# The gathered expert rows of the last token block, moved out of the building of the routing grid

## The chip, the core and the metric

One core of a Trainium2 chip runs the whole decoder layer in one launch. The metric is the time of one execution in device microseconds, and the median of three executions is compared. A span is the time from the first to the last instruction of one profiled execution, so that execution's own time lies a little above its span.

## The reference, cut to what matters

The layer runs a mixer of two attention branches, a cross-attention to memory tokens, and then the PEER expert layer, which is the part that the change touches. For each of the 512 tokens, 8 heads choose 16 of 16,384 experts each, by the 16 best sums of two 128-key scores. Expert e has a row of 1024 numbers in `u_tab` and one in `v_tab`; the token's dot product with the first, after a GELU and a softmax weight, scales the second.

```python
def peer_ffn(u, w_q, sub_keys, u_tab, v_tab):
    ...
    s = jnp.einsum('thcd,hcnd->thcn', q, sub_keys).astype(jnp.float32)
    top_s, top_i = lax.top_k(s, K)
    cand = (top_s[:, :, 0, :, None] + top_s[:, :, 1, None, :]).reshape(T, H, K * K)
    cand_i = (top_i[:, :, 0, :, None] * PEER_NKEYS + top_i[:, :, 1, None, :]).reshape(T, H, K * K)
    best_s, best_j = lax.top_k(cand, K)
    expert = jnp.take_along_axis(cand_i, best_j, axis=-1)
    g = jax.nn.softmax(best_s, axis=-1).astype(u.dtype)
    ...
        act = jax.nn.gelu(jnp.einsum('cd,chkd->chk', xc, u_tab[ec]), approximate=False)
        return jnp.einsum('chk,chkd->cd', gc * act, v_tab[ec])
```

The result goes through a final RMSNorm.

## The kernel before

The 512 tokens are four blocks of 128. The expert layer treats them in two ways.

**Blocks 0 to 2 are dense.** All 16,384 experts are computed for these 384 tokens, in 64 pairs of 2 x 128 experts. For one pair, the product with the U weights (`u_mm`, L675) takes 48 matmuls of 384 columns and the GELU follows; the result is multiplied by a weight that is zero where a token has not chosen the expert (`weigh`, L958), and the product with the V rows (`mm_V`, L964) takes 36 matmuls of 512 columns, which add up in six PSUM banks. Every float32 operand is split into a high and a low part first (`split`, L79: ScalarE casts the high part, then VectorE or GpSimd subtracts it).

The weights come from a routing grid of 128 x 128 numbers per token, which `build_G` (L833) makes: for 8 tokens at a time VectorE writes two one-hot matrices and two scaled ones (L872 to L875, `o` and `og`), TensorE multiplies them (L880), ScalarE copies them out (L882) and SyncE stores them in DRAM (L895). There are 48 such groups: 16 for each of three blocks. Before a block's grid can be built its chosen experts are decoded from the top-16 indices (`decode`, L752, a generator that gives way after each piece of VectorE and GpSimd work); `DECO` says beside which block of the grid which decode runs. `slots(b)` (L845) then transposes what the decode of block b left.

Beside the routing and the grid, the U products of 27 of the 64 pairs are computed ahead and kept in DRAM (`pre`, L694, tile `Ad`), one after every third group of the grid. What is left of them when the grid is done follows it.

**Block 3 is gathered.** Each of its 128 tokens has 128 chosen experts. `gather(n)` (L901) works through slots 0 to 255: for slots 0 to 127 a GpSimd indirect DMA (L907) fetches one U row for each of 128 tokens into one of four buffers `gt`, 512 KB in all, and VectorE takes the dot product (L909); after slot 127 come the GELU and the weights (L911, L912); for slots 128 to 255 the V rows are fetched in the same way and VectorE adds them up in `acc` (L914, L916). The indices `ex` are written at the end of the decode of block 3 (L794, L795). `self.gathered` counts the slots done.

**The dense experts' loop** (`experts`, L919) is written in the order in which each engine runs it. In step i:

```python
                weigh(i)
                o = mm_U(i + 1)
                load_V(i + 1)
                due = first + min(2 * P - first, (2 * P - first) * sum(cost[:i + 1]) // sum(cost[:steps - 1]))
                self.gather((self.gathered + due) // 2)
                load_U(i + 2)
                self.gather(due)
                ...
                mm_V(i)
```

`order` takes the pairs as 1, 0, 3, 2, and so on. `cost` is 1 for a pair whose U product is in `Ad` and 2 for one whose isn't; `first` is the number of slots gathered before the loop. So the rest of the 256 slots is spread over the steps by their cost, in two calls per step, and where pair i + 2 is in `Ad`, `load_U(i + 2)` puts no work on VectorE between the two calls.

The program up to this loop is ordered by a list scheduler with costs of its own, engine by engine; the loop is not reordered. Each engine runs its own instructions in order.

Of the kernel before, what the change touches and what calls it, by code (L numbers as in the profile page):

```python
# [21 lines left out]
P = 128  # L22
D = 1024
S = 512
NB = S // P
# [20 lines left out]
ORD = ()  # L46
PREN = 1
DECG = 1
DECO = ((1, 3), (2,), ())
GAT = (16, 3, 2)  # L50
PGP = tuple(range(0, 60, 3))
GB = 2
GS = 2.0 ** 15
# [9 lines left out]
class Kernel:  # L63
# [768 lines left out]
    def build_G(self, decode):  # L832


        nc = self.nc
        v = nc.vector
        T, C = 8, 32
        with ExitStack() as s3:
            pool = self.pool(s3, "g")

            it = pool.tile([P, P, 2], F16, name="it")
            v.tensor_copy(it, self.iota.unsqueeze(2).broadcast_to([P, P, 2]))
            itb = it.unsqueeze(1).broadcast_to([P, T // 2, P, 2])

            def slots(b):  # L845

                tr = []
                for src, dt in ((self.i12[:, 0, b, :], F16), (self.i12[:, 1, b, :], F16), (self.ew[:, b].rearrange("p h k -> p (h k)"), F32)):
                    pt = self.bank("pt")
                    nc.tensor.transpose(pt[:, 0:P], src, self.ident)  # L850
                    d = pool.tile([P, P], dt, tag=f"tr{len(tr)}", bufs=2, name=self.nm("tr"))
                    if dt == F32:
                        nc.scalar.activation(d, pt[:, 0:P], AF.Copy, scale=GS)
                    else:
                        nc.scalar.copy(d, pt[:, 0:P])
                    tr.append(d)
                gp = [pool.tile([P, P], F16, tag=f"gp{z}", bufs=2, name=self.nm("gp")) for z in range(2)]
                v.tensor_copy(gp[0], tr[2])
                v.tensor_tensor(gp[1], tr[2], gp[0], OP.subtract)
                return tr[0], tr[1], *gp  # L860

            n, seen = 0, []
            nxt = slots(0)
            for b in range(ND):
                i1, i2, *gp = nxt
                dec, nxt = [decode(z) for z in DECO[b]], None
                for c0 in range(0, P, C):
                    Gs = pool.tile([P, P, C], F32, tag="Gs", bufs=2, name=self.nm("Gs"))
                    for t0 in range(c0, c0 + C, T):
                        bc = lambda z: z[:, t0:t0 + T].rearrange("p (a b) -> p a b", b=2).unsqueeze(2).broadcast_to([P, T // 2, P, 2])  # L870
                        o1, o2, og1, og2 = (pool.tile([P, T // 2, P, 2], F16, tag=z, bufs=GB, name=self.nm(z)) for z in ("o1", "o2", "og1", "og2"))
                        v.tensor_tensor(o1, itb, bc(i1), OP.is_equal)  # L872
                        v.tensor_tensor(o2, itb, bc(i2), OP.is_equal)
                        v.tensor_tensor(og1, o1, bc(gp[0]), OP.mult)
                        v.tensor_tensor(og2, o1, bc(gp[1]), OP.mult)  # L875
                        for q0 in range(0, T, 4):
                            pg = self.bank(("pj", "po")[q0 // 4 % 2]).rearrange("p (q i) -> p q i", q=4)
                            for q in range(4):
                                for j, z in enumerate((og1, og2)):
                                    nc.tensor.matmul(pg[:, q, :], lhsT=o2[:, (q0 + q) // 2, :, q % 2], rhs=z[:, (q0 + q) // 2, :, q % 2], start=j == 0, stop=j == 1)  # L880
                            tt = t0 - c0 + q0
                            nc.scalar.activation(Gs[:, :, tt:tt + 4], pg.rearrange("p q i -> p i q"), AF.Copy, scale=1.0 / GS)  # L882
                        n += 1
                        if n % PREG == 0:
                            self.pre(nc.gpsimd if n // PREG in PGP else None)
                        if dec and n % DECG == 0 and next(dec[0], 1):
                            seen.append(DECO[b][-len(dec)])
                            if seen[-1] == b + 1:
                                nxt = slots(b + 1)
                            dec.pop(0)  # L890
                        if NB - 1 in seen and n > GAT[0] and n % GAT[1] == 0:
                            self.gather(min(P, self.gathered + GAT[2]))
                    gv = Gs.rearrange("j (q x) t -> j q (x t)", x=4)
                    for z in range(0, P // 4, 8):
                        nc.sync.dma_start(self.Gd[z:z + 8, :, (b * P + c0) // C].rearrange("q j x t -> j q (x t)"), gv[:, z:z + 8])  # L895
                assert not dec and (nxt or b == ND - 1)
            while self.pairs:
                self.pre()
# [203 lines left out]
```

## Time and profile before

| what | value |
|---|---|
| median of 3 executions | 1864.16 us (1862.62 to 1865.55) |
| the profiled execution's own time | 1866.06 us |
| its span | 1864.3 us |
| granted TensorE clock over the span | 0.981 |
| busy: PE, DVE, ACT, POOL | 1794.1, 1340.0, 746.5, 611.3 us |
| moved by DMA | 406.23 MB, of which 134.23 MB by the gathers' queue |
| first gather issued | 834.7 us |
| dense experts' loop on PE, first V product to last | about 1023 to 1856 us |

PE is TensorE, DVE VectorE, ACT ScalarE, POOL GpSimd and SP the engine that issues the other DMAs. A busy PE need not be a PE at its peak, since matmuls overlap; where it matters the starts of matmuls are read.

### The profile page before, as it was taken

What the parts mean: (1) busy time and instruction counts of PE and PEld (TensorE: products, weight loads), DVE (VectorE), ACT (ScalarE), POOL (GpSimd) and SP (SyncE); (2) the same over time, 40 slices, a digit from 0 to 9 for tenths busy, and PEclk for the clock granted to TensorE, in tenths of its full rate; (3) what the DMA queues carried; (4) which work ended last, traced back from release to release, by engine and by line L of the source; (5) the groups of instructions that cost most, each with busy time, mean ns of one, the idle gap of its engine ahead of it and who ended that gap; (6) DMA issues with size and microseconds to landing.
All of it is one profiled execution on the core that took longest, in us unless ns stands there. A gap on an engine that the chain in (4) does not pass through costs nothing.

```text
span 1864.3 us, 26137 instructions
## 1 busy us (share of the span) xinstructions
PE 1794.1 (96%) x9831; PEld 1570.8 (84%) x9831; DVE 1340.0 (72%) x2573; ACT 746.5 (40%) x1227; POOL 611.3 (33%) x403
## 2 busy tenths in 40 slices
PE   8999999999998999779998999999999999999998
PEld 7887776888977888779998888888888898899887
DVE  4454666456555999989994777777777787787877
ACT  4553455544453333334454332323323232332334
POOL 1212112100222344665300444444343434344442
PEclk8999999999998999899999999999999999999999
DMA  6422110044322234359998889888989898997994
GB/s 203 158 75 74 57 46 23 29 147 154 127 76 93 75 91 140 124 182 336 337 318 271 304 314 351 318 293 315 336 301 333 313 332 306 330 345 254 342 343 148
DMA packets 157247, 406.23 MB, mean 218 GB/s; under 512 B 12992, under 2 KB 62912, under 8 KB 156992
## 3 DMA queue, kind: packets, MB, share of 16 engines
q1 hardware_dynamic: 120256, 270.32, 41.7%
q0 software_dynamic: 36864, 134.23, 20.5%
q8 instruction: 77, 1.26, 0.3%
q14 instruction: 50, 0.41, 0.1%
HBM read 364.53 MB, written 38.93 MB: 216 GB/s over the span
## 4 chain that ended last, share of the span: by engine, by line
PE 74%; DVE 16%; issue 4%; POOL 3%; DMA 2%; ACT 1%; SPq 0%; POOLq 0%; ACTq 0%; DVEq 0%
PE pj L90 9%; PE pj L91 9%; PE pj L92 9%; PE sc L90 7%; PE sc L91 7%; PE sc L92 7%; PE po L90 4%; PE po L91 4%; PE po L92 4%; PE pt L91 3%; PE pt L92 3%; PE pt L90 3%; PE sc L183 2%; POOL doh L786 2%; DVE wl L81 2%
## 5 line engine op out<-in xcount | busy, mean ns | idle before, releaser
L90 PE MATMUL sc<-x3h,wh 128*128 128x384 f32 x1024 | 351.4, 343 | 3.2 <-ACT x3h L81 3.0
L91 PE MATMUL sc<-x3l,wh 128*128 128x384 f32 x1024 | 350.1, 342 | 1.9 <-DVE x3l L81 1.9
L92 PE MATMUL sc<-x3h,wl 128*128 128x384 f32 x1024 | 349.3, 342 | 0.0
L907 POOL DMA_INDIRECT gt<-in_peer_u,ex x128 | 192.3, 1502 | 341.7 <-DVE gt L909 319.5
L81 ACT CAST wh<-wr 128x1024 fp32r<-128x1024 f32 (+1 forms) x230 | 225.6, 1019 | 128.1 <-PE pj L91 38.8
L907 POOL DMA_INDIRECT gt<-in_peer_v,ex x128 | 187.8, 1468 | 263.3 <-DVE acc L916 232.3
L81 DVE TENSOR_TENSOR wl<-wr,wh 128x1024 fp32r<-128x1024 f32 (+2 forms) x176 | 206.7, 1202 | 68.0 <-ACT wh L81 67.8
L81 DVE TENSOR_TENSOR v<-vr,v 128x1024 fp32r<-128x1024 f32 x128 | 151.1, 1221 | 128.4 <-ACT v L81 128.4
L90 PEld LDWEIGHTS sc<-x3h,wh 128*128 128x128 f32 x1024 | 194.4, 190 | 5.6 <-ACT x3h L81 3.2
L91 PEld LDWEIGHTS sc<-x3l,wh 128*128 128x128 f32 x1024 | 194.8, 190 | 4.0 <-DVE x3l L81 2.3
L92 PEld LDWEIGHTS sc<-x3h,wl 128*128 128x128 f32 x1024 | 194.3, 190 | 0.3 <-DVE wl L81 0.2
L81 ACT CAST w<-ge 128x768 fp32r<-128x768 f32 x64 | 53.5, 835 | 337.8 <-DVE ge L960 320.5
L81 POOL TENSOR_TENSOR wl<-wr,wh 128x1024 fp32r<-128x1024 f32 x54 | 134.5, 2511 | 164.6 <-ACT wh L81 144.2
L81 ACT CAST v<-vr 128x1024 fp32r<-128x1024 f32 x128 | 128.0, 1049 | 116.3 <-PE pj L92 116.3
L916 DVE SCALAR_TENSOR_TENSOR acc<-gt,ag,acc 128x1024 f32<-128x1024 f32 x127 | 162.9, 1282 | 4.4 <-DMA gt<-in_peer_v,ex 1.8
L909 DVE SCALAR_TENSOR_TENSOR gt<-gt,xg 128x1024 f32<-128x1024 f32 x128 | 156.7, 1258 | 9.2 <-DMA gt<-in_peer_u,ex 9.2
L90 PE MATMUL po<-v,w 128*128 128x512 f32 x256 | 100.3, 392 | 6.1 <-ACT w L81 6.1
L90 PE MATMUL pj<-uh,wh 128*128 128x512 f32 x256 | 103.6, 405 | 0.3 <-ACT gates L466 0.3
L81 DVE TENSOR_TENSOR w<-ge,w 128x768 fp32r<-128x768 f32 x64 | 61.3, 958 | 57.8 <-ACT w L81 53.2
L91 PE MATMUL pj<-ul,wh 128*128 128x512 f32 x256 | 102.1, 399 | 0.0
L92 PE MATMUL pj<-uh,wl 128*128 128x512 f32 x256 | 102.0, 399 | 0.0
L92 PE MATMUL po<-v,w 128*128 128x512 f32 x256 | 100.9, 394 | 0.3 <-DVE w L81 0.3
(368 smaller groups left out, 3921.8 us busy)
## 6 DMA issues: line engine op xcount, KB each, us to landing
wr<-in_ut SPq DMA_DIRECT2D x128, 512.0 KB
vr<-in_peer_v SPq DMA_DIRECT2D x128, 512.0 KB
Gd<-Gs SPq DMA_DIRECT2D x48, 512.0 KB
G<-Gd SPq DMA_DIRECT2D x32, 768.0 KB
wr<-in_w_in SPq DMA_DIRECT2D x36, 512.0 KB
Ad<-ge SPq DMA_DIRECT2D x27, 384.0 KB
ge<-Ad SPq DMA_DIRECT2D x27, 384.0 KB
wr<-in_w_pq SPq DMA_DIRECT2D x16, 512.0 KB
```

What stands on the lines that cost most here:

```text
L81: return nc.scalar.copy(h, src), (eng or nc.vector).tensor_tensor(l, src, f32(h), OP.subtract)
L90: first = mm(out, lhsT=lh, rhs=rh, start=start, stop=False)
L91: mm(out, lhsT=lh, rhs=rl, start=False, stop=False)
L92: mm(out, lhsT=ll, rhs=rh, start=False, stop=stop)
L183: self.mark = nc.tensor.matmul(s, lhsT=q[x][:, bl], rhs=k[y][:, 0:n], start=(x, y) == (0, 0), stop=(x, y) == (1, 0))
L786: nc.gpsimd.tensor_tensor(oh, oh, tf[:, hs].unsqueeze(3).broadcast_to([P, 4, 16, 16]), OP.mult)
L907: nc.gpsimd.indirect_dma_start(g, None, tab, bass.IndirectOffsetOnAxis(ap=self.ex[:, s % P:s % P + 1], axis=0))
L909: v.scalar_tensor_tensor(g, g, 1.0, self.xg, OP.mult, OP.mult, accum_out=ag[:, s:s + 1])
L916: v.scalar_tensor_tensor(acc, g, ag[:, s - P:s - P + 1], acc, OP.mult, OP.add)
```

## The change

Block 3 is decoded beside block 2 of the grid instead of beside block 0, and the calls of `gather` inside `build_G` are taken out. Before, they were made at every third group from the 18th to the 48th, for two slots each: 11 calls, 22 slots. `first` becomes 0, and the loop over the dense experts gathers all 256 slots instead of 234.

```diff
-DECO = ((1, 3), (2,), ())
-GAT = (16, 3, 2)
+DECO = ((1,), (2,), (3,))
...
                             if seen[-1] == b + 1:
                                 nxt = slots(b + 1)
                             dec.pop(0)
-                        if NB - 1 in seen and n > GAT[0] and n % GAT[1] == 0:
-                            self.gather(min(P, self.gathered + GAT[2]))
```

Since the decode of block 3 now ends in block 2 of the grid, `seen[-1] == b + 1` holds there as well, and `slots(3)` is called: three transposes on PE, three copies on ACT and two small operations on DVE, whose results nobody reads.

The order of VectorE's instructions in the grid, at the place where the first gathered rows were used before (`gt`; `o` and `og` are the grid's, `wl` is the low part of U weights, `doh` and `i` belong to a decode; lines after the change are lower by 1 in the helper and the grid and by 3 from `gather` on):

```order
L872 TENSOR_TENSOR o_1213_7903<-it,tr_7307 128x1024
L776 TENSOR_TENSOR i_5253<-doh_8071 128x64
L909 SCALAR_TENSOR_TENSOR gt_8000,ag<-gt_8000,xg 128x1024
L909 SCALAR_TENSOR_TENSOR gt_8003,ag<-gt_8003,xg 128x1024
L873 TENSOR_TENSOR o_1201_7860<-it,tr_7311 128x1024
L874 TENSOR_TENSOR og_1202_7861<-o_1200_7859,gp_7317 128x1024
L875 TENSOR_TENSOR og_1203_7862<-o_1200_7859,gp_7318 128x1024
```

The same place after:

```order
L871 TENSOR_TENSOR o_1200_7852<-it,tr_7307 128x1024
L775 TENSOR_TENSOR i_5253<-doh_8930 128x64
L774 TENSOR_TENSOR doh_8970<-doh_8970 128x4x64
L873 TENSOR_TENSOR og_1189_7810<-o_1187_7808,gp_7317 128x1024
L872 TENSOR_TENSOR o_1188_7809<-it,tr_7311 128x1024
L874 TENSOR_TENSOR og_1190_7811<-o_1187_7808,gp_7318 128x1024
```

The 22 rows of L909 are gone from the grid's order; the decodes keep their places early in it.

VectorE in step 25 of the dense loop before, between the split of `v` and the weighing `ge`:

```order
L81 TENSOR_TENSOR v_12717<-vr_12722,v_12716 128x1024
L909 SCALAR_TENSOR_TENSOR gt_12726,ag<-gt_12726,xg 128x1024
L909 SCALAR_TENSOR_TENSOR gt_12729,ag<-gt_12729,xg 128x1024
L909 SCALAR_TENSOR_TENSOR gt_12732,ag<-gt_12732,xg 128x1024
L909 SCALAR_TENSOR_TENSOR gt_12735,ag<-gt_12735,xg 128x1024
L960 TENSOR_TENSOR ge_12660<-ge_12660,G_12658 128x768
```

The same step after:

```order
L80 TENSOR_TENSOR v_12691<-vr_12696,v_12690 128x1024
L906 SCALAR_TENSOR_TENSOR gt_12700,ag<-gt_12700,xg 128x1024
L906 SCALAR_TENSOR_TENSOR gt_12703,ag<-gt_12703,xg 128x1024
L906 SCALAR_TENSOR_TENSOR gt_12706,ag<-gt_12706,xg 128x1024
L906 SCALAR_TENSOR_TENSOR gt_12709,ag<-gt_12709,xg 128x1024
L906 SCALAR_TENSOR_TENSOR gt_12712,ag<-gt_12712,xg 128x1024
L906 SCALAR_TENSOR_TENSOR gt_12715,ag<-gt_12715,xg 128x1024
L957 TENSOR_TENSOR ge_12634<-ge_12634,G_12632 128x768
```

Four rows in a run become six. The whole order of DVE in the loop has runs of four or more at steps 13, 25, 39, 51 and 62: they are 5, 4, 4, 4 and 5 rows long before and 5, 6, 5, 6 and 6 after.

GpSimd's queue after the change, from the last decode on:

```order
L785 TENSOR_TENSOR doh_8970<-doh_8970,tf_8928 128x1024
L904 DMA gt_10136<-in_peer_u,ex 128x1024
L904 DMA gt_10139<-in_peer_u,ex 128x1024
L904 DMA gt_10152<-in_peer_u,ex 128x1024
L904 DMA gt_10155<-in_peer_u,ex 128x1024
L80 TENSOR_TENSOR wl_8866<-wr_8867,wh_8865 128x1024
```

The first four gathers still stand right behind the last decode, ahead of four splits of U weights; they fill the four buffers, and nothing reads them before the dense loop. On PE the order now has the equivalent of 21.4 of the 27 products computed ahead before the last grid matmul and 5.6 behind it; before it was 24.9 and 2.1.

## Rows read from the trace of the kernel before

**Rows 1.** The page's part 1: busy time of each engine over the span.

```profile
PE 1794.1 (96%) x9831; PEld 1570.8 (84%) x9831; DVE 1340.0 (72%) x2573; ACT 746.5 (40%) x1227; POOL 611.3 (33%) x403
```

**Rows 2.** Busy time by stretch; columns: stretch, length, engines, PEclk, DMA share, GB/s.

```profile
834.00:912.00 78.00, 74.03 (x569) 69.97 (x567) 78.00 (x118) 34.10 (x59) 39.62 (x24) 1.00 1.01 337
912.00:916.00 4.00, 3.54 (x22) 3.42 (x23) 4.00 (x8) 2.68 (x5) 1.14 (x1) 0.58 0.94 368
916.00:1018.00 102.00, 101.54 (x785) 98.26 (x783) 74.15 (x107) 46.19 (x79) 7.42 (x6) 1.00 0.95 302
1018.00:1024.00 6.00, 0.76 (x2) 0.50 (x2) 4.01 (x4) 3.60 (x5) 0.00 (x0) 0.82 0.58 197
1024.00:1853.00 829.00, 828.29 (x4020) 735.72 (x4019) 633.65 (x679) 280.28 (x344) 347.97 (x232) 1.00 0.86 312
```

**Rows 3.** PE's waits from 834 to 1018 us: total, times, longest.

```profile
PE pj L880 <- DVE og L874: 2.2, 3, 1.1
PE pj L880 <- DVE og L875: 1.9, 4, 0.8
```

**Rows 4.** Groups of DVE instructions from 834 to 1022 us: count, busy us, mean ns.

```profile
L909 DVE SCALAR_TENSOR_TENSOR gt<-gt,xg 128x1024 f32<-128x1024 f32 x22 | 31.7, 1448 | 0.0
L81 DVE TENSOR_TENSOR wl<-wr,wh 128x1024 fp32r<-128x1024 f32 x26 | 31.5, 1216 | 16.7 <-ACT wh L81 16.6
...
L872 DVE TENSOR_TENSOR o<-it,tr 128x1024 f16<-128x1024 f16 x35 | 23.4, 680 | 0.0
```

**Rows 5.** DVE's timeline in step 13: start, us, instruction, idle before and its releaser.

```profile
1195.18 1.22 DVE L909 SCALAR_TENSOR_TENSOR gt<-gt,xg 128x1024 f32<-128x1024 f32 x1
...
1198.62 1.22 DVE L909 SCALAR_TENSOR_TENSOR gt<-gt,xg 128x1024 f32<-128x1024 f32 x1
...
1205.86 1.23 DVE L909 SCALAR_TENSOR_TENSOR gt<-gt,xg 128x1024 f32<-128x1024 f32 x1 [6.02 <-DMA gt<-in_peer_u,ex]
...
1207.01 0.96 DVE L960 TENSOR_TENSOR ge<-ge,G 128x768 f32<-128x768 f32 x1
```

**Rows 6.** POOL's timeline at the same place.

```profile
1196.68 1.68 POOL L907 DMA_INDIRECT gt<-in_peer_u,ex  x1 [6.50 <-DVE gt L909]
1198.66 1.99 POOL L907 DMA_INDIRECT gt<-in_peer_u,ex  x1 [0.30 <-issue]
```

**Rows 7.** PE's timeline: V products of steps 13 and 14, then of 25 and 26.

```profile
1200.08 0.39 PE L90 MATMUL po<-v,w 128*128 128x512 f32 x1
...
1208.89 0.50 PE L90 MATMUL po<-v,w 128*128 128x512 f32 x1 [0.45 <-ACT w L81]
...
1217.74 0.35 PE L90 MATMUL sc<-x3h,wh 128*128 128x384 f32 x1
...
1358.84 0.39 PE L90 MATMUL po<-v,w 128*128 128x512 f32 x1
...
1375.20 0.35 PE L90 MATMUL sc<-x3h,wh 128*128 128x384 f32 x1
```

**Rows 8.** DVE's timeline in step 25: the weighing of step 26.

```profile
1359.56 0.96 DVE L960 TENSOR_TENSOR ge<-ge,G 128x768 f32<-128x768 f32 x1 [0.96 <-ACT ge L1018]
```

**Rows 9.** Timelines of PE, DVE and POOL in step 62, the last run of five.

```profile
1839.51 0.39 PE L90 MATMUL po<-v,w 128*128 128x512 f32 x1
...
1841.32 1.28 DVE L916 SCALAR_TENSOR_TENSOR acc<-gt,ag,acc 128x1024 f32<-128x1024 f32 x1 [1.47 <-DMA gt<-in_peer_v,ex]
1842.52 0.95 DVE L960 TENSOR_TENSOR ge<-ge,G 128x768 f32<-128x768 f32 x1
...
1836.16 1.86 POOL L907 DMA_INDIRECT gt<-in_peer_v,ex  x1 [5.88 <-DVE acc L916]
```

**Rows 10.** DVE's waits for gathered rows from 1024 to 1850 us: total, times, longest.

```profile
DVE gt L909 <- DMA gt<-in_peer_u,ex: 9.2, 4, 6.0
...
DVE acc L916 <- DMA gt<-in_peer_v,ex: 1.8, 2, 1.5
```

**Rows 11.** The page's part 5: the first half of the gathers on POOL.

```profile
L907 POOL DMA_INDIRECT gt<-in_peer_u,ex x128 | 192.3, 1502 | 341.7 <-DVE gt L909 319.5
```

**Rows 12.** Groups of PE instructions from 740 to 1020 us: two thirds of the `slots` transposes.

```profile
L850 PE MATMUL pt<-cB,i 128*128 128x128 f32 x6 | 1.9, 317 | 5.7 <-DVE i L776 5.7
```

## Prediction

> **What bounds the kernel now.** I read the page first, then the busy time by stretch around the place of the change, then who waits for whom, and last the timelines of the places where PE stops. PE is busy for 96% of the span [rows 1], so what the change is worth is the idle time of PE, and the time at the lower clock, that it takes away in one stage and brings in another.
>
> The stages are in [rows 2]. In the later part of the grid, from 834 to 912 us, the reader is to see DVE busy for all of 78.00 us and the DMA share at 1.01, while PE still reaches 74.03: DVE sets the pace and PE loses 3.97. Then, from 912 to 916, PEclk is 0.58: of its two levels, 2.4 and 1.2 GHz, the lower one was granted for most of this stretch, right behind the time in which PE had been waiting for DVE. From 916 to 1018 PE is busy for 101.54 of 102 while DVE idles: PE sets the pace. The 6 us from 1018 to 1024 are the hand-over to the dense loop, in which the first weighing waits for the GELU of its own pair; nothing in it depends on the gathers. In the dense loop, 829 us long, PE is busy for 828.29 at a clock of 1.00. It is the bound without any slack: a delay of PE there is added to the time. DVE is busy for 633.65 of the 829, POOL for 347.97, and the DMA share is 0.86.
>
> **Part 1, what leaves the grid.** The 22 products of gathered rows take 31.7 us of DVE between 834 and 1022 [rows 4], and 22 of the gathers leave POOL, 1.5 us each [rows 11]. DVE is behind PE only until 912, so the gain is what PE loses by it, not the 31.7. PE's waits for DVE's grid operands are 2.2 + 1.9 = 4.1 us [rows 3]. The fall of the clock cost 42% of 4 us, 1.7. The upper bound is 4.1 + 1.7 = 5.8. The lower bound is nothing, for this reason: the scheduler fills the room. By count in the whole order, only some 21.4 of the 27 products computed ahead stand before the last grid matmul, where 24.9 stood, and 5.6 follow it. So PE meets the grid's operands earlier too: a group of 8 tokens takes DVE four operations of 0.68 us or little less [rows 4], and PE has less of its own to do between two groups. I take about half, **-3.0 us**. A loss isn't excluded either, for with less work of its own PE could wait more often; I bound it by half of the present 4.1, 2 us.
>
> The decode of block 3 changes its block of the grid by the table; by the order it stays early, some 50 rows of DVE later. POOL's four multiplications and DVE's pieces for it are the same in number. I cost this at nothing: DVE's work before 834 us stays the same to a row or two, and if the cover went, it would be inside the bounds above. On SP only the stores of the grid and of the products computed ahead change places; no load of the dense loop moves.
>
> The four gathers that fill `gt` are still issued behind the last decode. They are ahead of four splits of U weights in POOL's queue, but so were the gathers of before, which waited there for DVE as well; the fifth, which must wait for DVE, stands behind the splits. So nobody waits for it.
>
> **Part 2, what is added.** `slots(3)` is dead work: three PE transposes of 0.317 us [rows 12], at most 1.0 us of PE, part of it overlapped. I take **+0.5**.
>
> **Part 3, what comes to the dense loop.** 22 more rows are gathered there. As a sum they fit: DVE gets 22 x 1.22 = 27 us on top of 633.65 [rows 2, 5], which makes 80% of 829; POOL 22 x 1.5 = 33 on top of 347.97; the DMA 22 x 0.524 = 11.5 MB, which is 14 GB/s on 312 and lifts the share of 0.86 to about 0.90. By totals nothing becomes the bound, and the edit would cost nothing.
>
> But the rows come in runs, and there are four buffers `gt`. Step 13 of before shows what a fifth row in a run costs. DVE starts the first of five products at 1195.18 and the fourth at 1198.62, back to back, 1.15 apart; the fifth starts at 1205.86, after 6.02 us of waiting for its row [rows 5]. That row could only be asked for when the first product had given back its buffer: POOL issued it at 1196.68 [rows 6], so it took 9.18 us from issue to use. The weighing behind it starts at 1207.01, and PE's V product of step 14 at 1208.89, 1.88 after the weighing [rows 5, 7]. What PE lost: the V products of steps 13 and 14 run from 1200.08 to 1217.74, which is 17.66, while those of steps 25 and 26, the same work, take 1375.20 - 1358.84 = 16.36 [rows 7]. So a run of five costs **1.30 us** of PE. Step 25 of before has a run of four: its next weighing starts at 1359.56 [rows 8], and the V product that needs it is due at 1358.84 + 8.18 = 1367.02, 5.6 us after the weights can be ready. No wait, no cost.
>
> After the change the runs at steps 25 and 51 grow from 4 to 6 and the one at step 39 from 4 to 5; step 13 keeps its 5. All lie at the same place, an even step whose pair was not computed ahead, with the same loads of V rows and U weights around them. Step 39 then costs 1.30. In a run of six the weighing comes later by one more product, 1.15 us, or, if the sixth row lags behind the fifth as its issue did, by 1198.66 - 1196.68 = 1.98 [rows 6]. The middle is 1.57, so a run of six costs 1.30 + 1.57 = 2.87. Sum: 1.30 + 2 x 2.87 = **+7.0 us**.
>
> The bounds of this term: from below nothing, if rows land sooner. Step 62 has a run of five too, and there the fifth row was issued at 1836.16 and used at 1841.32, 5.16 us later, with 1.47 of waiting [rows 9]; the weighing at 1842.52 was ready by 1844.4, and its V product due at 1839.51 + 8.18 = 1847.7. Such a landing costs PE nothing, and with a sixth row (1.15 to 1.98 later) still nothing. From above: if rows land as late as in step 13 at step 62 as well, that run of six is 4.0 + 1.98 us later against 3.3 to spare, another 2.7. I take step 13's price for the three inner steps, because loads of V rows and U weights run beside them as in step 13, while at step 62 only the last V rows are still to come; and step 62's own price for step 62.
>
> A rule speaks against this price. The Trainium skill, DMA: Bandwidth & Descriptors, section "Anatomy of one DMA — SWDGE (gpsimd) path", fits a GpSimd-issued DMA as 2.0 us plus its bytes at 436 GB/s: estimated from that page, 3.2 us for a gather of 512 KB. By it the fifth row would be there before the fourth product ends, runs would cost nothing, and the sum would be -2.5. The two rows here, 9.18 and 5.16 us beside other traffic, differ from it, so the measurement decides.
>
> Single rows elsewhere I cost at nothing: over the whole loop DVE waits for rows 9.2 + 1.8 us, of which 6.0 and 1.5 are the two cases above [rows 10], and PE idles 0.71 us in all [rows 2]. What hides them is that DVE is ahead of PE by some us at every other step; each step has on average a third of a row more, 0.4 us.
>
> **Sum:** -3.0 + 0.5 + 7.0 = +4.5 us, on the profiled execution's 1866.06 us: 1870.6. That execution is 1.9 above the median of the runs shown, so against the median it is **1868.7 us**, slower by 0.24%. About 0.2%, 3.7 us, is what a measurement of this kernel can tell from no change.
>
> **Rivals.**
> - *The rows land in time (faster).* In steps 25, 39 and 51 rows take 5.2 us, as in step 62 [rows 9], not 9.2. The point that decides is the wait for the fifth row: V product 14 was due at 1200.08 + 8.18 = 1208.26 and came 0.63 late after a wait of 6.02 [rows 5, 7], so a run of five is free with a wait below 5.4, and one of six, with its 1.15 to 1.98 more, below 3.4 to 4.2. With 1.5, as in step 62, all of the 7.0 is gone. What is left is -2.5, or -5.3 with the full gain in the grid: 1858.9 to 1861.7. For it: only 6.02 of the 11 us of waits in the loop is of the long kind. Against: that one is the only run of five in the middle of the loop.
> - *The clock falls in the two long stops.* The stops at steps 26 and 52 would be 2 to 3 us long. A fall of the clock like that of 912 to 916 [rows 2], with 1.7 us lost, at each gives +3.4: 1872.1. For it: before that fall no single wait had been above 1.1 us [rows 3]. Against: in the loop PE works without pause on both sides of a stop, and the stop at 1208 brought no fall. [...]
> - *The DMA falls behind.* With the share near 0.90 and 5 or 6 rows in every second step, waits like step 13's appear at ordinary steps too. 4 to 8 further stops of 1.30 give +5 to +10: 1874 to 1879. For it: at a share of 1.01 in the grid PE did lose time [rows 2]. Against: 0.86 at present with 0.71 us idle.
> - *It cancels.* The grid gives its full 5.8, and stops cost 5 to 7: within 0.2%. The same if the change does little of what it says, since four of the rows are still fetched during the grid.
>
> **How the numbers follow.** My forecast has 0.50: with the grid between 0 and -5.8 and the runs between 5 and 9 it spans 1865 to 1872, of which 0.30 is above 1867.9 and 0.20 below. Rows in time: 0.17, of which 0.13 is faster by over 0.2% and 0.04 within. Clock: 0.15, DMA: 0.10, both slower. Cancelling: 0.08. So slower 0.55, same 0.32, faster 0.13. The range from 1860 to 1876 takes in most of the faster rival, all of the clock's and the first half of the DMA's; about 0.15 is left out. The likeliest case's own range is 1865 to 1872.
>
> **What would show it.** In the profile after: no L909 row before the dense loop, DVE idle in the later grid, PE waiting less than 4 us there and no stretch at a lower clock around 912; a longer stretch of U products alone between grid and loop; the hand-over, now from 1018 to 1024 [rows 2], some 2 to 4 us earlier. In the loop: DVE waits of 4 to 6 us for rows at steps 13, 25, 39 and 51 and hardly elsewhere, and PE's V products of steps 25-26 and 51-52 about 19 us long, of 39-40 about 17.7, instead of 16.36. I am wrong if those four waits aren't there, if PE's idle time in the loop is below 2 us or above 12, or if the loop begins more than 6 us earlier.

## The result, and the profile after

The changed kernel takes **1882.88 us** (median of 4 runs, 1880.71 to 1888.66) against 1863.39 for the kernel before (1861.67 to 1865.55, 4 runs on the same chip). The ratio is 1.011 with a 95% interval from 1.0095 to 1.0125: slower by about 19 us, where 1868.7 and at most 1876 were forecast. The profiled execution took 1882.05 us, its span 1880.3 stands against 1864.3 before: 16.0 us more. (Before, the profiled execution, 1866.06, lay 2.7 us above the median; this one lies 0.8 below. So the spans differ by 3.5 us less than the medians, and what follows accounts for the 16.0.)

In what follows a line number of the changed kernel is one less than before for helpers and grid, and three less from `gather` on (L909 is now L906, L907 is L904, L960 is L957).

The page's part 1, which answers to [rows 1]. The totals hardly show it: PE is busy for 5 us more, DVE for as long as before.

```profile
PE 1799.5 (96%) x9834; PEld 1571.9 (84%) x9834; DVE 1339.0 (71%) x2575; ACT 744.5 (40%) x1230; POOL 618.6 (33%) x403
```

Busy time by stretch, which answers to [rows 2] (columns as there); the last four rows are two stops in the loop and what follows each.

```profile
834.00:912.00 78.00, 75.99 (x656) 71.94 (x655) 74.69 (x115) 40.98 (x75) 24.15 (x9) 1.00 0.92 287
912.00:916.00 4.00, 4.00 (x41) 3.75 (x40) 4.00 (x8) 1.95 (x3) 0.00 (x0) 1.00 0.84 246
...
1024.00:1866.00 842.00, 828.77 (x3997) 731.99 (x3996) 652.59 (x710) 273.17 (x334) 376.84 (x253) 0.99 0.88 318
1365.00:1369.00 4.00, 0.97 (x4) 0.30 (x2) 2.88 (x4) 1.64 (x2) 1.64 (x2) 1.00 0.69 241
1369.00:1373.00 4.00, 3.76 (x10) 2.98 (x11) 4.00 (x6) 2.98 (x4) 0.05 (x1) 0.57 0.70 226
1714.00:1718.00 4.00, 0.80 (x4) 0.34 (x2) 2.15 (x2) 0.70 (x1) 2.27 (x2) 0.95 0.76 267
1718.00:1725.00 7.00, 6.82 (x17) 5.16 (x18) 6.80 (x6) 3.92 (x5) 1.94 (x2) 0.54 0.51 157
```

The grid did get faster: PE's loss from 834 to 912 is 2.01 us instead of 3.97, and from 912 to 916 the clock stays at 1.00. PE's waits in that stretch, which answer to [rows 3], fell from 4.1 us to 1.8:

```profile
PE po L89 <- ACT w L80: 5.7, 1, 5.7
PE pj L879 <- DVE o L872: 1.1, 4, 0.4
PE pj L879 <- DVE og L874: 0.7, 2, 0.4
```

(The first row is the hand-over.) No product of a gathered row stands there any more; the first starts at 1021.41, and the 22 of [rows 4] are in the loop. The first V product of the dense loop starts at 1018.21, where it started at 1023.24 before: **5.0 us won**.

```profile
1018.21 0.80 PE L89 MATMUL po<-v,w 128*128 128x512 f32 x1 [5.69 <-ACT w L80]
```

The loop then loses **19.4 us**: from the first V product to the start of the last V matmul PE takes 851.81 us instead of 832.41. In [rows 2] PE idled 0.71 of 829 us; above it idles 13.2 of 842, and after two stops the clock is at its lower level for most of 4 and 7 us. DVE's waits for rows from 1024 to 1866 us, which answer to [rows 10], went from 11.0 us in 6 waits to 54.8 in 28:

```profile
DVE gt L906 <- DMA gt<-in_peer_u,ex: 33.7, 20, 6.2
DVE acc L913 <- DMA gt<-in_peer_v,ex: 21.1, 8, 6.2
```

DVE's timeline in step 25, now a run of six, which answers to [rows 5]; then POOL's, which answers to [rows 6], and PE's, to [rows 7].

```profile
1351.97 1.22 DVE L906 SCALAR_TENSOR_TENSOR gt<-gt,xg 128x1024 f32<-128x1024 f32 x1
...
1355.41 1.22 DVE L906 SCALAR_TENSOR_TENSOR gt<-gt,xg 128x1024 f32<-128x1024 f32 x1
...
1362.80 1.23 DVE L906 SCALAR_TENSOR_TENSOR gt<-gt,xg 128x1024 f32<-128x1024 f32 x1 [6.16 <-DMA gt<-in_peer_u,ex]
...
1365.23 1.23 DVE L906 SCALAR_TENSOR_TENSOR gt<-gt,xg 128x1024 f32<-128x1024 f32 x1 [1.20 <-DMA gt<-in_peer_u,ex]
...
1366.38 0.95 DVE L957 TENSOR_TENSOR ge<-ge,G 128x768 f32<-128x768 f32 x1
```

```profile
1353.47 1.68 POOL L904 DMA_INDIRECT gt<-in_peer_u,ex  x1 [6.11 <-DVE gt L906]
1355.46 1.98 POOL L904 DMA_INDIRECT gt<-in_peer_u,ex  x1 [0.30 <-issue]
```

```profile
1356.87 0.39 PE L89 MATMUL po<-v,w 128*128 128x512 f32 x1
...
1368.25 0.50 PE L89 MATMUL po<-v,w 128*128 128x512 f32 x1 [3.01 <-ACT w L80]
...
1369.71 0.63 PE L89 MATMUL po<-v,w 128*128 128x512 f32 x1
...
1378.68 0.35 PE L89 MATMUL sc<-x3h,wh 128*128 128x384 f32 x1
```

The fifth row is used 9.33 us after its issue (1362.80 less 1353.47), as in step 13 of before (9.18), and the sixth comes 2.43 us behind it. PE stands for 3.0 us, and a matmul behind the stop takes 0.63 instead of 0.39: the lower clock of the table above. The V block of steps 25 and 26 takes 1378.68 less 1356.87, 21.81 us, against 16.36 in [rows 7]: 5.45 lost.

The same reading, block by block (a V block is 8.18 us per step, a U block 8.46, where nothing stops), adds up to the whole difference of the spans, but for rounding:

| place | forecast, us | measured, us |
|---|---|---|
| start of the loop (grid, `slots(3)`) | -2.5 | -5.0 |
| first V block, behind the hand-over | 0 | -1.1 |
| runs of five: step 39 (13 is one before too) | 1.30 (0) | 2.11 (0.17) |
| runs of six: steps 25, 51 | 2.87 each | 5.45, 6.65 |
| three rows, a `wl` split, three rows: steps 22, 48 | 0 | 3.12, 2.29 |
| step 7 | 0 | 0.75 |
| behind the last V matmul's start | 0 | 1.6 |
| sum | 4.5 | 16.0 |

The -1.1 is the lower clock of the hand-over, which now lay more on the wait and less on the block behind it: PEclk is 0.59 from 1018 to 1022 us, before it was 0.57 from 1021 to 1029.

What steps 22 and 48 have is no run without a split. DVE's timeline in step 22 shows that four buffers are too few there too. (Steps 14 and 40 have the same three rows, split, three rows; there DVE waits 1.5 and 0.7 us for the last row, and PE loses nothing.)

```profile
1309.67 1.22 DVE L906 SCALAR_TENSOR_TENSOR gt<-gt,xg 128x1024 f32<-128x1024 f32 x1
...
1310.82 2.35 DVE L80 TENSOR_TENSOR wl<-wr,wh 128x1024 fp32r<-128x1024 f32 x2
1313.09 1.22 DVE L906 SCALAR_TENSOR_TENSOR gt<-gt,xg 128x1024 f32<-128x1024 f32 x1
...
1315.28 1.23 DVE L906 SCALAR_TENSOR_TENSOR gt<-gt,xg 128x1024 f32<-128x1024 f32 x1 [0.96 <-DMA gt<-in_peer_u,ex]
...
1319.87 1.23 DVE L906 SCALAR_TENSOR_TENSOR gt<-gt,xg 128x1024 f32<-128x1024 f32 x1 [3.35 <-DMA gt<-in_peer_u,ex]
```

PE's stop behind it lasts 2.28 us, and that of step 51's run of six 3.38:

```profile
1322.89 0.50 PE L89 MATMUL po<-v,w 128*128 128x512 f32 x1 [2.28 <-ACT w L80]
...
1718.18 0.80 PE L89 MATMUL po<-v,w 128*128 128x512 f32 x1 [3.38 <-ACT w L80]
```

In step 62, now also a run of six, PE never stops, but DVE comes out later, and after the last V products it is DVE's chain of final additions that ends the kernel. This answers to [rows 9]:

```profile
1855.81 1.28 DVE L913 SCALAR_TENSOR_TENSOR acc<-gt,ag,acc 128x1024 f32<-128x1024 f32 x1 [1.53 <-DMA gt<-in_peer_v,ex]
...
1858.32 1.28 DVE L913 SCALAR_TENSOR_TENSOR acc<-gt,ag,acc 128x1024 f32<-128x1024 f32 x1 [1.23 <-DMA gt<-in_peer_v,ex]
...
1859.53 0.95 DVE L957 TENSOR_TENSOR ge<-ge,G 128x768 f32<-128x768 f32 x1
```

This weighing begins 10.5 us ahead of the last V matmul (1870.02), before it was 13.1 (1855.64 less 1842.52).

### The profile page after: what moved, and what is told of

It is laid out like the page before. It is cut to its first block, busy times and chain, and to the rows that moved or that the text cites. A ratio compares the mean times of both kernels' runs of the same rounds, so it can differ in the third digit from the quotient of the medians.

```text
span 1880.3 us, 26185 instructions
## 1 busy us (share of the span) xinstructions
PE 1799.5 (96%) x9834; PEld 1571.9 (84%) x9834; DVE 1339.0 (71%) x2575; ACT 744.5 (40%) x1230; POOL 618.6 (33%) x403
## 5 line engine op out<-in xcount | busy, mean ns | idle before, releaser
L904 POOL DMA_INDIRECT gt<-in_peer_u,ex x128 | 198.9, 1554 | 353.0 <-DVE gt L906 314.7
L904 POOL DMA_INDIRECT gt<-in_peer_v,ex x128 | 187.1, 1462 | 235.2 <-DVE acc L913 203.1
L906 DVE SCALAR_TENSOR_TENSOR gt<-gt,xg 128x1024 f32<-128x1024 f32 x128 | 152.1, 1220 | 33.9 <-DMA gt<-in_peer_u,ex 33.7
```

The source lines that it names most:

```text
L904: nc.gpsimd.indirect_dma_start(g, None, tab, bass.IndirectOffsetOnAxis(ap=self.ex[:, s % P:s % P + 1], axis=0))
L906: v.scalar_tensor_tensor(g, g, 1.0, self.xg, OP.mult, OP.mult, accum_out=ag[:, s:s + 1])
```

## The experiments

**The theory**: a row's way takes 9 us in the middle of the loop, and a fifth row can only be asked for when the first has been used; where more than four rows are wanted within that time, DVE waits, the weighing is late and PE stops. **The rivals**: the DMA engines are behind as a whole (share 0.88 against 0.86); rows in the loop cost in proportion; the decoding's place is at work. The times below are medians; the ratios are against runs of the kernel before on the same chip.

### Six buffers

```
-            g = self.gep.tile([P, D], F32, tag="gt", bufs=4, name=self.nm("gt"))
+            if s % 6 == 5:
+                g = self.i12.rearrange("p c b k -> p (c b k)")
+            else:
+                g = self.gx.tile([P, D], F32, tag="gt", bufs=5, name=self.nm("gt"))
...
+        self.gx = self.pool(s1, "gx")
...
-        gF = self.row_gain(gp, "g_fin")
+        gF = None
...
+                if i == steps - 2:
+                    gF = self.wp.tile([P, D], F32, tag="wr", bufs=3, name=self.nm("g_fin"))
+                    nc.sync.dma_start(gF, a["g_fin"].unsqueeze(0).broadcast_to([P, D]))
```

`i12` holds the decoded keys and is dead in the loop; the final gain's 4 KB per partition moved into a tile that is free at the end, to make room.

> The changed kernel with six buffers for gathered rows instead of four (five in the loop's own pool, the sixth is the dead index tile), so that a fifth and a sixth row are asked for six rows ahead. Theory (runs of rows against the buffers): the waits of 5.9 to 6.2 us at steps 13, 25, 39 and 51 and those of 3 us at steps 22 and 48 fall under 1.5 us each, PE's stops at V blocks 25, 39, 51 go, TensorE's clock stays up in the loop, and the loop from the first V product to the last takes 834 to 840 us instead of 852.0: 1864 to 1870 us. Rival (the DMA engines are behind, whatever is asked for early comes late): the waits move to other rows, the loop keeps 848 us or more, 1878 us or more.

Measured: **1860.06 us** (1859.33 to 1861.38), ratio 0.9977 [0.9967, 0.9986], so faster than the kernel before. The loop takes 830.86 us, less than the theory's 834 to 840, and the time lies below its 1864 to 1870. From 1024 to 1848 us PE is busy without a gap, at a DMA share of 0.89:

```profile
1024.00:1848.00 824.00, 824.00 (x4012) 732.78 (x4011) 655.09 (x719) 278.92 (x341) 384.74 (x252) 1.00 0.89 325
```

Among DVE's waits in the loop none is for a row any more; these are all:

```profile
DVE v L80 <- ACT v L80: 106.7, 34, 5.9
DVE w L80 <- ACT w L80: 56.8, 63, 0.9
DVE h L983 <- PE po L91: 1.0, 1, 1.0
DVE ge L961 <- ACT ge L1022: 0.8, 1, 0.8
DVE ag L912 <- ACT ag L911: 0.4, 1, 0.4
```

All 22 rows and all their bytes are still in the loop. So the whole of the 19.4 us hung on when a row could be asked for. The time behind the last V matmul's start is 8.66 us, that of before (8.65), so the 1.6 us at the end went too.

### Five buffers

```
-            g = self.gep.tile([P, D], F32, tag="gt", bufs=4, name=self.nm("gt"))
+            if s % 5 == 4:
+                g = self.i12.rearrange("p c b k -> p (c b k)")
+            else:
+                g = self.gep.tile([P, D], F32, tag="gt", bufs=4, name=self.nm("gt"))
```

> The changed kernel with one more buffer only: every fifth row goes into the dead index tile, the other four buffers as they are. Theory: in the changed kernel a fifth row is asked for when the first has been used and is there 9.3 us after, with three rows of 1.15 us in between (wait 5.9 to 6.2 us measured). With five buffers the fifth row is free (steps 13, 39), and a sixth (25, 51) has four rows in between: 9.3 less 4.6, a wait of some 4.7 us in place of 7.4, which leaves PE a stop of 0.5 to 1.5 us and the clock up. Loop 833 to 837 us, time 1863 to 1868 us, waits for rows 10 to 25 us in all. Rival (the six-buffer kernel won by where its buffers lie or by its first row of five before the loop, not by their number): 1872 us or more.

Measured: 1863.74 us (1861.74 to 1866.46), ratio 1.0 [0.9991, 1.001], loop 834.70. Runs of five are free. A run of six now behaves as one of five did: one wait, and a short stop of PE. DVE's and PE's timelines at step 25 (from `gather` on, lines are three higher here than in the changed kernel):

```profile
1358.04 1.23 DVE L909 SCALAR_TENSOR_TENSOR gt<-gt,xg 128x1024 f32<-128x1024 f32 x1 [5.39 <-DMA gt<-in_peer_u,ex]
```

```profile
1361.06 0.50 PE L89 MATMUL po<-v,w 128*128 128x512 f32 x1 [0.96 <-ACT w L80]
```

The V blocks of 25-26 and 51-52 lose 1.84 and 1.60, and no others lose anything to speak of. The clock stays up in the loop. Waits for rows are 10.1 us in all.

### A cap on the rows of a step

```
+                if i < steps - 2:
+                    due = min(due, self.gathered + (4 if order[i + 2] in self.Ad else 5))
                 self.gather((self.gathered + due) // 2)
```

> The changed kernel with its four buffers, but a step takes at most 4 rows where the two halves stand without a wl split between them and at most 5 elsewhere; what is over goes to the next step (six steps differ from the changed kernel: 13, 25, 39, 51 lose one or two rows, 22 and 48 one). Same bytes, same number of rows in the loop. Theory (runs of rows): the stops of PE at steps 13, 22, 25, 39, 48, 51, some 19 us in all with the lost clock, fall to 5 us or less: 1863 to 1869 us. Rival (DMA load): no more than 4 us are won, 1878 us or more. Step 14, 26, 40, 52 begin with a late start; if a carried row only moves the stop there, 1872 to 1878.

Measured: 1871.57 us (1866.42 to 1872.51), ratio 1.0042 [1.0029, 1.0054]; the profiled execution, among the fastest, has a loop of 837.34, which is 14.5 less than the changed kernel's. The stops at 13, 22, 25, 39, 48 and 51 are gone, more than the rival allows, yet the median lies above the theory's range and just under the last case's. Eight steps give rows up and not six, for 14 and 40 were over five too. In part the carried row moves the stop: blocks 15-16, 27-28 and 43-44 lose 1.32, 1.57 and 0.66. DVE's waits for rows from 1024 to 1852 us are now many and short:

```profile
DVE gt L906 <- DMA gt<-in_peer_u,ex: 24.2, 23, 2.5
DVE acc L913 <- DMA gt<-in_peer_v,ex: 16.8, 23, 1.7
```

By the ratios, 1.0042 against 1.011, spreading alone brings back about three fifths of the loss; six buffers bring back all of it.

### Half of the change

```
-GAT = (16, 3, 2)
+GAT = (16, 3, 1)
```

(In the kernel before: 11 rows are gathered in the grid instead of 22.)

> Half of the change: the grid gathers 11 rows instead of 22 (one where it gathered two), four buffers, the rest in the loop. By the due formula the runs without a split are 5 rows at steps 13, 25, 39, 51 and 62 (the kernel before 5, 4, 4, 4, 5; the changed kernel 5, 6, 5, 6, 6), and no step has 3 rows on both sides. Theory (runs): four stops of 1.3 to 1.5 us, the loop 4 to 5 us longer than before's 832.5, clock never down in it; the grid half faster, 2 us: 1864 to 1868 us. Rival (rows in the loop cost in proportion): half of 19.4 us less 2: 1870 to 1873 us.

Measured: 1868.01 us (1866.62 to 1869.71), ratio 1.0021 [1.0011, 1.0031], at the upper end of the theory's range; loop 837.61, 5.2 over before, where 4 to 5 were expected. The four runs of five lose 1.35, 1.15, 1.36 and 1.05 us, so the forecast's price of 1.30 was right here; another 1.64 comes at steps 11 and 12, which it didn't hold. The cost goes by runs and not by rows: the first 11 rows cost 5.2 us of loop, the next 11 cost 14.2.

### More traffic alone

```
                 load_V(i + 1)
+                if i % 3 == 0:
+                    nc.sync.dma_start(self.i12.rearrange("p c b k -> p (c b k)"), a["peer_v"][i * P:(i + 1) * P, :])
```

> The kernel before, with 22 plain transfers of 512 KB more in the loop (one in every third step, into a dead tile, nobody reads them): the change's traffic without its rows on VectorE. Theory (runs of rows against four buffers): the runs are those of the kernel before, so PE's stops stay near 1.3 us in all, at most 4 us more than before: 1862 to 1867 us. Rival (DMA load): most of the 19 us that the loop lost come with the bytes: 1873 us or more.

Measured: 1863.86 us (1861.84 to 1865.77), ratio 0.9999 [0.9989, 1.0008]. Loop 832.59, where before had 832.41. The DMA share is 0.89, more than the changed kernel's 0.88, and PE hardly loses:

```profile
1024.00:1853.00 829.00, 828.38 (x4020) 735.57 (x4020) 633.87 (x679) 280.61 (x344) 347.24 (x232) 1.00 0.89 325
```

The rival by the DMA's total load falls, as far as transfers spread over the loop can show it.

### The decoding's place

```
-DECO = ((1,), (2,), (3,))
+DECO = ((1, 3), (2,), ())
```

(In the changed kernel; `slots(3)` falls away with it.)

> Only one part of the change: no row is gathered in the grid, but the last block is decoded in the first block of the grid as before (so its transposes are not in the grid either). Theory (the gathers carry everything, the decoding's place is worth 0.5 us): the loop as in the changed kernel, 850 to 854 us, its start within 1.5 us of the changed kernel's 1018.3, time 1880 to 1885 us. Rival (part of the 4.9 us that the grid won comes from decoding in even thirds): the loop begins 2 us or more later, at 1020.5 or after, time 1885 or more.

Measured: 1881.96 us (1878.09 to 1884.75), ratio 1.0101 [1.0079, 1.0123]. The loop takes 852.38 and begins at 1016.40, earlier and not later, by a little more than the 1.5 us allowed. A single start says little: in five other runs with the changed kernel's grid the loop began between 1016.2 and 1020.8, and with the old decoding and six buffers (the last run below) at 1020.82. On average the two starts with the old decoding, 1018.6, are those of the changed grid, 1018.5. So the rival falls, and what the grid won is the gathers' leaving.

### What a row's way is made of

In the trace's packet records the fifth row of step 25 has its first packet 5.1 us after the issue began and its last 8.3 after, and it is used at 9.3. At step 62, where hardly another load is left, these are 2.6, 4.8 and 5.2. Two runs take transfers away from beside it.

```
                 for x in range(2):
-                    r = pw.tile([P, D], F32, tag="vr", bufs=3, name=self.nm("vr"))
-                    nc.sync.dma_start(r, a["peer_v"][(2 * order[i] + x) * P:(2 * order[i] + x + 1) * P, :])
+                    if x == 0:
+                        r = pw.tile([P, D], F32, tag="vr", bufs=3, name=self.nm("vr"))
+                        nc.sync.dma_start(r, a["peer_v"][2 * order[i] * P:(2 * order[i] + 1) * P, :])
```

> The changed kernel without the second of the two V transfers of each step (64 of 128 transfers of 512 KB; the second half is split from the first half's tile, so half of the dense experts' value table is left out). All runs of rows and all splits stay. It asks why a row takes 9.3 to 9.9 us from its issue to its use at steps 13, 25, 39, 51. Theory A (it shares 16 busy DMA engines with the V and U tables): with a third of the traffic gone a row needs 4 to 6 us, the fifth row's wait falls from 6.2 to under 3 us, PE stops at V blocks 25 and 51 lose at least half: 1862 to 1872 us. Theory B (issue on GpSimd and a fixed way to memory): waits stay at 5.5 us or more, 1878 us or more.

Measured: 1872.24 us (1869.32 to 1874.57), ratio 1.0052 [1.0038, 1.0066]. The fifth row takes 8.1, 7.3 and 7.9 us at steps 13, 25 and 51, between the two theories, and the time lies just over theory A's edge. The cut took a ninth of the loop's traffic, not a third as expected: 284 GB/s from 1024 to 1853 us, against the 318 above. It settled nothing by itself, so the second run takes all of them:

```
-                    r = pw.tile([P, D], F32, tag="vr", bufs=3, name=self.nm("vr"))
-                    nc.sync.dma_start(r, a["peer_v"][(2 * order[i] + x) * P:(2 * order[i] + x + 1) * P, :])
-                    self.split(V[i][0][:, x, :], V[i][1][:, x, :], r)
+                    self.split(V[i][0][:, x, :], V[i][1][:, x, :], self.xg)
```

> The changed kernel with none of the dense loop's V transfers (128 of 512 KB; V is split from a tile that is in SBUF already, so the dense experts' value table is left out of the result). Runs of rows, splits and buffers stay. With half of these transfers the fifth row took 8.1, 7.3 and 7.9 us from issue to use at steps 13, 25, 51 instead of 9.35, 9.3, 9.6; at step 62, with hardly any other load left, 5.2. Theory (the V loads that the split sets off stand ahead of the fifth row): 5.0 to 6.0 us at all four places, waits of 1.5 to 3 us there, no stop of PE and no low clock at V blocks 25, 39, 51: 1856 to 1863 us. Rival (most of the 9.3 us is the row's own way): 7 us or more, waits of 3.5 us or more.

Measured: 1871.16 us (1866.14 to 1876.60), ratio 1.0034 [1.002, 1.0048]. The fifth row now takes 5.9, 5.8, 6.2 and 5.1 us at steps 13, 25, 51 and 62, within 0.2 us of what the theory has. Two rows in DVE's and POOL's timelines, the first in step 22 and the second in step 25 (1363.74 less 1357.96 is 5.78):

```profile
1322.74 1.23 DVE L906 SCALAR_TENSOR_TENSOR gt<-gt,xg 128x1024 f32<-128x1024 f32 x1 [5.23 <-DMA gt<-in_peer_u,ex]
...
1363.74 1.22 DVE L906 SCALAR_TENSOR_TENSOR gt<-gt,xg 128x1024 f32<-128x1024 f32 x1 [2.61 <-DMA gt<-in_peer_u,ex]
```

```profile
1312.91 1.98 POOL L904 DMA_INDIRECT gt<-in_peer_u,ex  x1 [0.30 <-issue]
...
1357.96 1.68 POOL L904 DMA_INDIRECT gt<-in_peer_u,ex  x1 [6.54 <-DVE gt L906]
```

The losses of blocks 25-26 and 51-52, 5.45 and 6.65 us, are 0.5 and 0.1. But the time is not what was expected, for the sixth row of step 22, the first of each pair above, takes 9.83 us (1322.74 less 1312.91), and that of step 48 takes 8.6. The losses around steps 22 and 48 grew to 5.6 and 4.6 us. In each, PE stops, for 3.1 and 1.9 us, and the clock falls behind the stop. The stop at step 48 and the 4 us after it:

```profile
1670.77 0.50 PE L89 MATMUL po<-v,w 128*128 128x512 f32 x1 [1.89 <-ACT w L80]
```

```profile
1672.00:1676.00 4.00, 4.00 (x12) 3.08 (x12) 4.00 (x4) 3.27 (x5) 0.47 (x1) 0.57 0.31 117
```

No V load runs beside the sixth rows of steps 22 and 48; the loads of U weights do, but no run took those away, so what delays these two rows stays open.

### What the change is worth when no row waits

The kernel before gets six buffers too: its four, the dead `i12` and a spare tile, the two used for every fifth and sixth row of the loop.

```
+            z = (s - self.loop0) % 6 if self.loop0 else 0
+            if z > 3:
+                g = (self.i12.rearrange("p c b k -> p (c b k)"), self.spare)[z - 4]
+            else:
+                g = self.gep.tile([P, D], F32, tag="gt", bufs=4, name=self.nm("gt"))
```

(Cut: `spare` is a tile of the loop's own pool, `loop0` the first slot gathered in the loop, and the final gain moved as with six buffers.)

> The kernel before (22 rows in the grid) with six buffers for the rows of the loop. It is the fair partner of the changed kernel with six buffers (1860.06 us): the difference is what the change wins in the grid when no row waits in the loop. Theory: the loop loses the 1.3 us of step 13, its start stays at 1022 to 1024 us: 1861 to 1863.5 us, 1 to 3.5 us over the changed kernel with six buffers. Rival (the grid's win comes back in the loop in any case, since 22 rows more take VectorE's time): 1860 us or less, no difference.

Measured: 1862.72 us (1859.22 to 1864.84), ratio 0.9991 [0.9981, 1.0]; the loop takes 831.03 and begins at 1022.89. The partner with the change had 1860.06, loop 830.86 from 1019.53. The two ran on different chips, so the ratios count: 0.9977 against 0.9991, some 2.6 us for gathering all rows in the loop once it has the buffers, with intervals that just overlap. The loops take the same, so what is won lies before them. The last run takes the old decoding beside that.

```
-DECO = ((1,), (2,), (3,))
+DECO = ((1, 3), (2,), ())
```

(In the changed kernel with six buffers.)

> The changed kernel with six buffers and the last block decoded in the first third as before: the best of both. In the run with the old decoding alone the loop began at 1016.4 us instead of 1018.2 to 1019.5. If that is the decoding's place: 1857 to 1859 us. If it is what two executions differ by: 1859.5 to 1861 us.

Measured: **1858.87 us** (1856.34 to 1862.15), ratio 0.9972 [0.9963, 0.9982], the fastest of all here. It lies in the range named for the decoding's place, but its interval overlaps with that of the six buffers alone, and its profiled execution began the loop at 1020.82, not early: whether the decoding's place is worth 1 us is undecided.

## Why the prediction was right and wrong

- **The mechanism** was right: four buffers, rows in runs, the weighing late, PE stopped. The waits of 5.9 to 6.2 us stand at steps 13, 25, 39 and 51, where they were forecast. The six buffers show that they carry the loss.
- **The step that failed** is the price of a run of six, "1.30 + 1.57 = 2.87". It measured 5.45 and 6.65. Most of the difference is the clock. It fell after both stops, and the prediction kept that apart as a rival with a chance of 0.15. That rival was no alternative; it belonged to the price, since it needs nothing but the stops that the forecast itself put there. By the two stretches (PEclk 0.57 over 4 us, 0.54 over 7) it cost 1.7 and 3.2 us, 4.9 in all against the 3.4 given. Without it 3.7 and 3.4 us are left, still over 2.87. The sixth row is used 2.43 and 2.42 us behind the fifth (steps 25 and 51), beyond the bounds of 1.15 to 1.98. At step 25 its issue lags by 1.99 and its last packet by 1.8, so the rest comes between the last packet and the use. The base of 1.30 isn't fixed either: the run of five at step 39 cost 2.11, with a fifth row that took 9.90 us instead of 9.18. The Trainium skill, TensorE: Matmul & The Clock Gate, section "HAM oscillation — how this bites in real kernels", tells of a loop whose waits for a DMA, some 3 to 5 us each, bring the lower clock back in every round. The stops of 3.0 and 3.4 us agree with it. The stop of 1.9 us in the run without V transfers is shorter, and the clock fell all the same; after the one of 2.28 us above it didn't.
- **"Single rows elsewhere I cost at nothing"** failed as well. Steps 22 and 48 (three rows, a split, three rows) and step 7 cost 6.2 us. The prediction counted runs by the row of code between them; the wait goes by the time between a row's use and the use of the row four places on, and a split of 2.3 us inside it doesn't always cover a way of 8 or 9.
- **The rival "the DMA falls behind"** saw these waits (28 instead of 6), but by a cause that isn't there: the same bytes without the rows cost nothing.
- **Rows in time, by the page on GpSimd's DMAs**: the Trainium skill, DMA: Bandwidth & Descriptors, section "Anatomy of one DMA — SWDGE (gpsimd) path", has a fixed 2.0 us and the bytes at 436 GB/s, an estimated 3.2 us for a row; the least seen for a row that DVE waited for was 4.6 (in the run with more traffic, 1344.01 less 1339.39), and in the runs of five and six in the middle of the loop 9.3 to 9.9. The trace doesn't agree, and the prediction was right to take the row. (3.2 us after its issue at 1196.68 the fifth row of step 13 would be there at 1199.88, as the fourth product ends at 1199.84 and not before it; the run would cost nothing all the same.)
- **The grid**: -2.5 was forecast with `slots(3)`; the loop began 5.0 earlier, inside the bounds. With the five other runs of the same grid it began at 1018.5 on average, and three runs with the grid of before began it at 1022.9, so 4.4 us hold; the half change began it at 1021.3, between them. The -3.0 was half of 5.8, the waits of 4.1 and the clock's 1.7. Of the waits 2.3 went (4.1 less 1.8), which is about half, but the clock's fall went whole: it stands at 912 us in all three profiles with the grid of before and in none of the nine others.
- **The tail**, 1.6 us, was not in the sum. PE's idle time in the loop of 13.2 us is over the 12 named as a sign of being wrong.
- **Slips that change nothing**: steps 13, 25, 39 and 51 are odd, and it is their pairs that are even; and the ends named for the grid and the runs, 0 to -5.8 and 5 to 9, give 1863.9 to 1873.7 with the 0.5 of `slots(3)`, more than 1865 to 1872.

## What to carry to other kernels

Count a stream's buffers against the time from asking to use: with n buffers the row n places on is asked for only when this one has been used, so more than n uses within one such time make a wait, whatever the mean load is. When a wait is priced for an engine that never pauses, price with it what its clock does after the stop, and don't set the two apart as alternatives. Before work is moved to a place with room in the totals, look for the fullest step there; here one more buffer took away the 19 us of loss (ratio 1.0), and two made a small win of it (0.9977).

## What was not expected of the hardware

- Of a row's way of 9.3 us at step 25, 3.5 came with the V loads: it was 5.8 once they were gone, and the first packet came 2.4 us after the issue began instead of 5.1. But 22 more transfers spread over the loop (share 0.89) changed nothing of the time. That the load just ahead counts and not the mean fits both; no run moved the same bytes to another place, so it is not shown by itself.
- The clock did not go by the length of a stop alone. After stops of 3.0 and 3.4 us in the changed kernel it was at 1.2 GHz for some us, and after PE's wait of 2.3 us at step 22 it was not (PEclk 1.00 from 1322 to 1330); but in the run without V transfers a stop of 1.9 us brought it down (0.57 from 1672 to 1676). Where all stops of the loop were 1.0 us or less (five buffers, the cap, half of the change) it stayed at 2.4.
